# Conditioning chunks and sample-state outputs as fp32 products in quarters of the array's columns

## The chip, the cores and the metric

One core of one Trainium2 chip runs the whole program. The metric is the device time of one execution in microseconds; the kernel before is shown with the median of three executions. One further execution was profiled, and all rows below are of it.

## The reference, cut to what matters

One layer of a conditioned hybrid decoder (RG-LRU and gated linear attention side by side, merged by gates, then a SwiGLU block) is computed for a prompt of 1024 tokens and for eight sample sequences of four tokens. Two places matter here.

The conditioning: each of the nine sequences (one prompt, eight samples) has a vector `c`, from which six vectors of 1024 modulate the layer:

```
mod = silu(c) @ ada_w + ada_b                  # (9, 1024) @ (1024, 6144)
sh1, sc1, gt1, sh2, sc2, gt2 = split(mod, 6)
h  = rmsnorm(x, norm1_g) * (1 + sc1) + sh1
...
x  = x + gt1 * (m @ w_out)
h2 = rmsnorm(x, norm2_g) * (1 + sc2) + sh2
x  = x + gt2 * (ffn(h2))
```

The sample sequences' attention output, per head, from a state `S` that each of the eight sequences brings along (128 x 256 for each head), with four tokens each:

```
o = att @ v + (q * exp(b)) @ S                 # per sequence: (4, 128) @ (128, 256)
S = exp(b_last) * S + (k * exp(b_last - b)).T @ v
```

## The kernel before, in words

The 1056 token rows are worked in two halves: A (512 prompt rows) and B (512 prompt rows and the 32 sample rows). Features lie on the 128 partitions, tokens along the free dimension. Every large product takes its weights as a tile of 128 x 1024 fp32 that is split in two fp32r parts: `load_w` (L121) loads the raw tile through the SP queue into one of three `raw` buffers, ScalarE writes the high part (L125), VectorE the remainder (L126), into one of three `hl` buffers. A product is then three fp32r products (L358 to L360).

The conditioning is cut into twelve chunks of 512 outputs, each with four weight tiles of 128 x 1024 (two contraction tiles of 512 columns in each). Chunks 2, 0, 3 and 1 are needed first and are made at the start by `ada_first` (L169): the raw fp32 tiles go into `S` buffers (pool `sbig`, 17 of them, shared with most of the large intermediate tiles), and each of the eight contraction tiles is one fp32 product of 32 stationary columns against 512 moving ones, written to one of four 32-partition quarters of a PSUM bank (L178). ScalarE copies the bank out (L181), and four products with a 0/1 matrix `sel` add the four quarters and transpose (L184); VectorE adds the bias (L186).

The other eight chunks (4 to 11) are made by `ada_chunk` (L218) with split weights through `load_w`, against a stationary `cst` of 128 columns that holds the high part of the conditioning in columns 0 to 8 and its remainder in 32 to 40 (`ada_split`, L208; `cst` keeps one `S` buffer): sixteen fp32r products of 512 columns (L226), a copy (L196), four transposes (L198), two VectorE operations (L201, L202).

Python generators set the order of the work. `ada_rest` (L244) runs chunks 4 to 11 one after the other and gives a step at each `yield`: five for a chunk, 40 in all. `weave` (L300) lets one or two such steps follow each tile of another generator: one after each step of `qk(1)` and of `values(1)`, two after each of the eight tiles of `r_tiles` (L798), and one at each step of `merge_b` (L935). `mix` (L310) then lays these fillers between the steps of the attention generator `gla` (L565), by the credits that the yields state. This happens in half A alone. Instructions of one engine run in the order in which they stand, the DMA issues of the SP queue too. PSUM banks for short use come from `ax` (L79), a pool of two.

In half B, `gla` makes the sample part for each of four heads: two loads bring the states (L746, `s0b`, two `S` buffers); eight fp32 products, one for each sequence, of 32 stationary columns (`qmb`) against 256 state columns add up in one 32-row PSUM area (L751), and one of 32 rows for the sequences' own tokens is added (L752). ScalarE copies out (L754), two transposes follow (L766), ScalarE copies the result into `ob` (L767). Between them stand the products for the new state (L758) and VectorE's update (L762).

Of the kernel before, what the change touches and what calls it, by code (L numbers as in the profile page):

```python
# [9 lines left out]
I32 = mybir.dt.int32  # L10
AF = mybir.ActivationFunctionType
OP = mybir.AluOpType
PSUM = bass.MemoryType.PSUM

P = 128
# [31 lines left out]
def hybrid_layer(ctx, tc, I, O):  # L47
# [11 lines left out]
    def S(name, dt=F32):  # L59
        return sbig.tile([P, 2 * 544], dt, tag="S", name=name)  # L60
# [29 lines left out]
    pool.dma_start(lmask, I["lmask"])  # L90
    bmask = cp.tile([P, NB], F32, name="bmask")
    pool.dma_start(bmask, I["bmask"])
    sel = cp.tile([P, 9], F32, name="sel")
    pool.dma_start(sel, I["sel"])
    hlru0 = cp.tile([P, NR, NB], F32, name="hlru0")
    pool.dma_start(hlru0, I["slru"])
    sconv = cp.tile([P, NR, NB, 3], F32, name="sconv")
# [68 lines left out]
    act.activation(cth[:, :, 0:9], ct, AF.Tanh, scale=0.5)  # L166
    dve.scalar_tensor_tensor(cth[:, :, 0:9], cth[:, :, 0:9], 1.0, ct, op0=OP.add, op1=OP.mult)

    def ada_first(cc):  # L169

        ps = ax(f"adaps{cc}")
        for kk in range(4):
            raw = S(f"ada{cc}{kk}")
            sp.dma_start(raw[:, :1024], I["ada_w"][cc, kk])
            for i in range(2):
                kt = 2 * kk + i
                g = 32 * (kt % 4)
                pe.matmul(ps[g:g + 32, :], cth[:, kt, :], raw[:, i * 512:(i + 1) * 512], start=(kt < 4), stop=(kt >= 4))  # L178
            yield 1.0
        row = T(f"adar{cc}")  # L180
        act.activation(row[:, :512], ps, AF.Copy)  # L181
        tps = ax(f"adat{cc}")
        for i in range(4):
            pe.matmul(tps[:, i * 16:i * 16 + 9], row[:, i * P:(i + 1) * P], sel, start=True, stop=True)  # L184
        mo = mod[:, 4 * cc:4 * cc + 4, :]
        dve.scalar_tensor_tensor(mo, tps[:, :64].rearrange("p (j m) -> p j m", m=16)[:, :, 0:9], 0.5, ada_bias(cc),  # L186
                                 op0=OP.mult, op1=OP.add)
        ada_derive(cc, mo)
        yield 1.0

    def ada_bias(cc):
        return bc(vec[:, V_ADAB + 4 * cc:V_ADAB + 4 * cc + 4].unsqueeze(2), [P, 4, 9])

    def ada_out(cc, ps, tps, row):
        n = 41
        act.activation(row[:n, :512], ps[:n], AF.Copy)  # L196
        for i in range(4):
            pe.transpose(tps[:, i * 64:i * 64 + n], row[:n, i * P:(i + 1) * P], ident[:n, :n])  # L198
        t3 = tps[:, :256].rearrange("p (j m) -> p j m", m=64)
        mo = mod[:, 4 * cc:4 * cc + 4, :]  # L200
        dve.scalar_tensor_tensor(mo, t3[:, :, 0:9], 0.5, ada_bias(cc), op0=OP.mult, op1=OP.add)  # L201
        dve.scalar_tensor_tensor(mo, t3[:, :, 32:41], 0.5, mo, op0=OP.mult, op1=OP.add)  # L202
        ada_derive(cc, mo)


    cst = []

    def ada_split():  # L208
        zz = S("zz")
        pool.memset(zz, 0.0)  # L210
        cw = S("cst", F32R)
        dve.tensor_copy(cw, zz)
        c3 = cw[:, :KD * P].rearrange("p (k m) -> p k m", m=P)
        dve.tensor_copy(c3[:, :, 0:9], cth[:, :, 0:9])
        dve.tensor_sub(c3[:, :, 32:41], cth[:, :, 0:9], c3[:, :, 0:9].bitcast(F32))
        cst.extend(c3[:, i, :] for i in range(KD))

    def ada_chunk(cc):  # L218

        ps = ax(f"adaps{cc}")  # L220
        for kk in range(4):
            w = load_w(I["ada_w"][cc, kk], 1024, f"ada{cc}{kk}")
            for i in range(2):
                kt = 2 * kk + i
                for u in range(2):
                    pe.matmul(ps, cst[kt], w[:, u, i * 512:(i + 1) * 512], start=(kt == 0 and u == 0),  # L226
                              stop=(kt == KD - 1 and u == 1))
            yield 0.87
        yield 0.5
        ada_out(cc, ps, ax(f"adat{cc}"), T(f"adar{cc}"))  # L230

    def ada_derive(cc, mo):
        ch, j = cc // 2, 4 * (cc % 2)
# [86 lines left out]
    class Half:  # L320
# [129 lines left out]
        def norm1(s):  # L450
            box = s.rb1
            s.h = []
            for q in range(2):
                if s.hf == 0 and q:
                    s.lr_half(0)
                    for i, t in enumerate((T_Q, T_Q + 1, T_K, T_K + 1)):
                        hl = load_w(I["w_in"][t], 1024, f"early{t}") if i < 3 else load_apart(I["w_in"][t], f"early{t}")
                        ps = mm(f"early{t}")
                        s.gemm(ps, hl, 4, s.h, 0, True, False)
                        s.early[t] = ps, hl  # L460
                    for cc in (3, 1):
                        yield from ada_first(cc)
                yield from s.modulate(s.h, s.xs, box[0], s.whole, range(4 * q, 4 * q + 4), 0, 0, "1" + s.n)


# [99 lines left out]
        def gla(s, pr, z, q, k, vg, vts):  # L565
# [125 lines left out]
            for i in range(2):  # L691
# [33 lines left out]
                if s.hf:  # L725
                    pool.dma_start(O["gla_p"][:, h, :], st_prev)
                    vs = vts[2 * i + 1]
                    kr = tp.tile([P, 4, NS], F32R, tag="vr", name=f"kr{n}{i}", bufs=2)
                    kes = bc(ke[:, i * N + HP:i * N + N].unsqueeze(1), [P, 2, NS])
                    dve.tensor_copy(kr[:, 0:2, :], kes)  # L730
                    dve.tensor_sub(kr[:, 2:4, :], kes, kr[:, 0:2, :].bitcast(F32))
                    qt = T(f"qm{n}{i}")
                    qm = qt[:, :NB * NS].rearrange("p (b j) -> p b j", b=NB)
                    dve.memset(qm, 0.0)
                    dve.tensor_copy(qt[:, :NB * 36].rearrange("p (b j) -> p b j", j=36)[:, :, 0:TS],
                                    qe[:, i * N + HP:i * N + N].rearrange("p (b j) -> p b j", j=TS))
                    yield 1
                    tps = ax(f"ktq{n}{i}")
                    pe.transpose(tps[:, :P], kr.rearrange("p a b -> p (a b)").bitcast(F32), ident)
                    kem = S(f"kem{n}{i}", F32R)  # L740
                    dve.tensor_mul(kem[:, :1024].rearrange("p (b k) -> p b k", b=NB), bc(tps[:, :P].unsqueeze(1), [P, NB, P]),
                                   bc(bmask.unsqueeze(2), [P, NB, P]))
                    sts = []
                    for g in range(2):
                        s0 = S(f"s0{n}{i}{g}")
                        sp.dma_start(s0[:, :1024], I["sgla"][h, :, g * 1024:(g + 1) * 1024])  # L746
                        sts.append(s0)
                    yield 2
                    pos = ax(f"pos{n}{i}")
                    for b in range(NB):  # L750
                        pe.matmul(pos[:NS, :256], qm[:, b, :], sts[b // 4][:, (b % 4) * 256:(b % 4 + 1) * 256], start=(b == 0), stop=False)  # L751
                    pe.matmul(pos[:NS, :256], atts[:, i * NS:(i + 1) * NS], vs[0], start=False, stop=True)  # L752
                    osb = T(f"osb{n}{i}")[:NS, :256]
                    act.activation(osb, pos[:NS, :256], AF.Copy)  # L754
                    for b in range(0, NB, 2):
                        ups = ax(f"upt{n}{i}{b}")
                        for d in range(2):
                            pe.matmul(ups[:, d * 256:(d + 1) * 256], kem[:, (b + d) * P:(b + d + 1) * P], vs[1], start=True, stop=True)  # L758
                        for d in range(2):
                            sv = sts[(b + d) // 4][:, ((b + d) % 4) * 256:((b + d) % 4 + 1) * 256]  # L760
                            ec = i * N + HP + (b + d) * TS + TS - 1
                            dve.scalar_tensor_tensor(sv, sv, e0[:, ec:ec + 1], ups[:, d * 256:(d + 1) * 256], op0=OP.mult, op1=OP.add)  # L762
                        yield 1
                    pot = ax(f"pot{n}{i}")
                    for v in range(2):
                        pe.transpose(pot[:, v * NS:(v + 1) * NS], osb[:, v * P:(v + 1) * P], ident[:NS, :NS])  # L766
                    act.activation(o3[:, :, HP:], pot[:, :2 * NS].rearrange("p (v j) -> p v j", v=2), AF.Copy)  # L767
                    for g in range(2):
                        pool.dma_start(O["gla_s"][h, :, g * 1024:(g + 1) * 1024], sts[g][:, :1024])
                os_.append(ot)  # L770
# [364 lines left out]
    mm_pool(1)  # L1135
    A.load_x()
    drain(A.norm1_sum())
    drain(ada_first(2))
    drain(ada_first(0))
    drain(A.norm1())  # L1140
    ada_split()
    derive()
    A.branches(None)
    up1 = A.ffn1(1)
# [41 lines left out]
def _pack(inp):  # L1186
# [40 lines left out]
    jj = np.arange(P)[:, None]  # L1227
    ii = np.arange(64)[None, :]
    a["lmask"] = np.stack([((jj // (2 * b) == ii // b) & (jj % (2 * b) < b)) for b in LEVELS], 1).astype(np.float32)
    a["sel"] = (np.arange(P)[:, None] % 32 == np.arange(9)[None, :]).astype(np.float32)  # L1230
    a["bmask"] = (np.arange(P)[:, None] % NS // TS == np.arange(NB)[None, :]).astype(np.float32)
    return a

# [27 lines left out]
```

## Time and profile before

| | |
|---|---|
| median of 3 executions | 2069.88 us (2068.68 to 2071.18) |
| the profiled execution | 2071.19 us |
| its span, first to last instruction | 2069.4 us |
| mean granted TensorE clock | 0.993 |
| PE / PEld busy | 2022.4 / 1835.9 us |
| VectorE (DVE) / ScalarE (ACT) busy | 1132.5 / 831.5 us |
| DMA | 228.39 MB, mean 110 GB/s |

Times are microseconds from the first instruction unless marked ns. PE is TensorE's products, PEld its weight loads, POOL is GpSimd, SP the queue that issues most loads. A product's recorded duration includes the time in which its last columns leave the array, so the distance from one start to the next is what it costs. fp32 products stand as two instructions each, fp32r products and transposes as one.

### The profile page before, as it was taken

How to read it: one execution, taken by the hardware profiler on the slowest of the kernel's cores; microseconds unless marked ns; L12 is line 12 of the kernel's file. 1: busy time of each engine (PE TensorE's matmuls, PEld its weight loads, DVE VectorE, ACT ScalarE, POOL GpSimd, SP SyncE). 2: the span in 40 equal slices, each digit the busy share in tenths (PEclk: the TensorE clock that was granted, in tenths of full speed). 3: DMA queues.
4: the chain of work that ended last, by engine and by line, in shares of the span. 5: the costliest groups of instructions: out<-in, count | busy, mean ns of one | idle time of the engine just before them, and what ended most of it. 6: DMA issues, size and time to landing. Idle time of an engine off the chain costs nothing. (4 is left out here: it accounts for less than half of the span.)

```text
span 2069.4 us, 31495 instructions
## 1 busy us (share of the span) xinstructions
PE 2022.4 (98%) x13106; PEld 1835.9 (89%) x13106; DVE 1132.5 (55%) x1795; ACT 831.5 (40%) x1153; POOL 85.3 (4%) x136
## 2 busy tenths in 40 slices
PE   6999999999999999999999999999999999999997
PEld 4787887788899888888899898899999999999997
DVE  4757767655347433446564597684243673333356
ACT  3536456645235322233352345563232442212232
POOL 1101001000000000000010011110000000000000
PEclk9999999999999999999999999999999999999999
DMA  7233423433344423342422313322233542232234
GB/s 284 79 111 94 138 76 116 134 122 110 98 154 148 133 79 105 102 139 72 152 69 85 115 48 105 107 78 96 79 96 99 166 136 94 75 107 86 90 114 126
DMA packets 74270, 228.39 MB, mean 110 GB/s; under 512 B 8496, under 2 KB 16304, under 8 KB 74128
## 3 DMA queue, kind: packets, MB, share of 16 engines
q1 hardware_dynamic: 70960, 216.98, 32.6%
q0 software_dynamic: 2624, 8.85, 1.2%
q8 instruction: 103, 1.69, 0.3%
q10 hardware_dynamic: 544, 0.56, 0.1%
q14 instruction: 39, 0.32, 0.0%
HBM read 217.12 MB, written 9.23 MB: 109 GB/s over the span
## 5 line engine op out<-in xcount | busy, mean ns | idle before, releaser
L360 PE MATMUL f3psb<-fab,f3b_hl 128*128 128x272 f32 x352 | 101.4, 288 | 0.0
L358 PE MATMUL f3psb<-fab,f3b_hl 128*128 128x272 f32 x352 | 101.3, 288 | 0.0
L359 PE MATMUL f3psb<-fab,f3b_hl 128*128 128x272 f32 x352 | 100.9, 287 | 0.0
L125 ACT ACTIVATE f3b_hl<-f3b_raw 128x768 fp32r<-128x768 f32 (+1 forms) x45 | 35.7, 793 | 88.4 <-PE f3psb L360 56.1
L358 PE MATMUL f3psa<-faa,f3a_hl 128*128 128x512 f32 x176 | 68.7, 390 | 0.0
L360 PE MATMUL f3psa<-faa,f3a_hl 128*128 128x512 f32 x176 | 68.5, 389 | 0.0
L359 PE MATMUL f3psa<-faa,f3a_hl 128*128 128x512 f32 x176 | 68.5, 389 | 0.0
L358 PEld LDWEIGHTS f3psb<-fab,f3b_hl 128*128 128x128 f32 x352 | 66.4, 189 | 0.0
L360 PEld LDWEIGHTS f3psb<-fab,f3b_hl 128*128 128x128 f32 x352 | 66.2, 188 | 0.0
L359 PEld LDWEIGHTS f3psb<-fab,f3b_hl 128*128 128x128 f32 x352 | 66.1, 188 | 0.0
L126 DVE TENSOR_TENSOR f3b_hl<-f3b_raw,f3b_hl 128x768 fp32r<-128x768 f32 (+1 forms) x45 | 40.1, 892 | 35.1 <-ACT f3b_hl L125 34.9
L125 ACT ACTIVATE f3a_hl<-f3a_raw 128x768 fp32r<-128x768 f32 (+1 forms) x32 | 25.4, 793 | 84.2 <-PE f3psa L360 46.4
L126 DVE TENSOR_TENSOR ada_hl<-ada_raw,ada_hl 128x1024 fp32r<-128x1024 f32 x32 | 38.9, 1222 | 24.8 <-ACT ada_hl L125 24.6
L126 DVE TENSOR_TENSOR f3a_hl<-f3a_raw,f3a_hl 128x768 fp32r<-128x768 f32 (+1 forms) x32 | 28.5, 890 | 39.0 <-ACT f3a_hl L125 38.3
L125 ACT ACTIVATE ada_hl<-ada_raw 128x1024 fp32r<-128x1024 f32 x32 | 33.5, 1054 | 35.6 <-PE vpsa L360 13.1
L358 PE MATMUL uxpsb<-h1b,uxpsb_hl 128*128 128x272 f32 x160 | 47.4, 296 | 0.0
L360 PE MATMUL uxpsb<-h1b,uxpsb_hl 128*128 128x272 f32 x160 | 46.2, 289 | 0.0
L358 PE MATMUL ugpsb<-h1b,ugpsb_hl 128*128 128x272 f32 x160 | 46.2, 289 | 0.0
L359 PE MATMUL uxpsb<-h1b,uxpsb_hl 128*128 128x272 f32 x160 | 46.1, 288 | 0.0
L360 PE MATMUL ugpsb<-h1b,ugpsb_hl 128*128 128x272 f32 x160 | 46.0, 288 | 0.0
L359 PE MATMUL ugpsb<-h1b,ugpsb_hl 128*128 128x272 f32 x160 | 45.8, 286 | 0.0
L360 PEld LDWEIGHTS f3psa<-faa,f3a_hl 128*128 128x128 f32 x176 | 33.0, 188 | 7.1 <-DVE f3a_hl L126 0.2
(1491 smaller groups left out, 7248.5 us busy)
## 6 DMA issues: line engine op xcount, KB each, us to landing
ada_raw<-in_ada_w SPq DMA_DIRECT2D x32, 512.0 KB, 3.6
f3b_raw<-in_ffn SPq DMA_DIRECT2D x23, 384.0 KB, 3.1
ada<-in_ada_w SPq DMA_DIRECT2D x16, 512.0 KB, 10.0
f3b_raw<-in_ffn SPq DMA_DIRECT2D x22, 320.0 KB, 2.9
woa_raw<-in_w_out SPq DMA_DIRECT2D x13, 512.0 KB, 3.4
wob_raw<-in_w_out SPq DMA_DIRECT2D x13, 512.0 KB, 3.3
f3a_raw<-in_ffn SPq DMA_DIRECT2D x16, 384.0 KB, 3.1
uxpsa_raw<-in_w_in SPq DMA_DIRECT2D x10, 512.0 KB, 3.6
```

The costliest lines, as they stand in the source:

```text
L125: act.activation(hl[:, 0, :n], raw[:, :n], AF.Copy)
L126: dve.tensor_sub(hl[:, 1, :n], raw[:, :n], hl[:, 0, :n].bitcast(F32))
L358: pe.matmul(out, wh, x[:, o:o + w], start=st, stop=False)
L359: pe.matmul(out, wh, x[:, N + o:N + o + w], start=False, stop=False)
L360: pe.matmul(out, wl, x[:, o:o + w], start=False, stop=en)
```

## The change

`ada_first` and the old `ada_chunk` become one `ada_chunk`, used for all twelve chunks: raw fp32 tiles in `S` buffers, loaded two at a time, eight fp32 products in quarters for each chunk, a copy of the bank, four transposes of 128 x 128, a VectorE reduction over the four quarters, and one VectorE operation for the bias. `cst`, `ada_split` and `sel` are gone. A chunk has three steps in place of five. The sample-state products go to four quarters in the same way (sequence b to quarter b mod 4, the own-token product to the last), and the quarters are added by a VectorE reduction after the transposes in place of ScalarE's copy.

```diff
-    sel = cp.tile([P, 9], F32, name="sel")
-    pool.dma_start(sel, I["sel"])
...
-    def ada_first(cc):
...
+    def groups(t, n):
+
+        return t.rearrange("p (j g m) -> p j m g", g=4, m=32)[:, :, 0:n, :]
+
+    def ada_load(cc, k0, k1):
+        raws = []
+        for kk in range(k0, k1):
             raw = S(f"ada{cc}{kk}")
             sp.dma_start(raw[:, :1024], I["ada_w"][cc, kk])
+            raws.append(raw)
+        return raws
+
+    def ada_chunk(cc, raws=None):
+
+        ps = ax(f"adaps{cc}")
+        for kk in range(0, 4, 2):
+            two = raws[kk:kk + 2] if raws else ada_load(cc, kk, kk + 2)
+            for g in range(4):
+                pe.matmul(ps[32 * g:32 * g + 32, :], cth[:, 2 * kk + g, :], two[g // 2][:, (g % 2) * 512:(g % 2 + 1) * 512],
+                          start=(kk == 0), stop=(kk == 2))
             yield 1.0
         row = T(f"adar{cc}")
         act.activation(row[:, :512], ps, AF.Copy)
         tps = ax(f"adat{cc}")
         for i in range(4):
-            pe.matmul(tps[:, i * 16:i * 16 + 9], row[:, i * P:(i + 1) * P], sel, start=True, stop=True)
+            pe.transpose(tps[:, i * P:(i + 1) * P], row[:, i * P:(i + 1) * P], ident)
         mo = mod[:, 4 * cc:4 * cc + 4, :]
-        dve.scalar_tensor_tensor(mo, tps[:, :64].rearrange("p (j m) -> p j m", m=16)[:, :, 0:9], 0.5, ada_bias(cc),
+        dve.tensor_reduce(mo, groups(tps, 9), axis=AX.X, op=OP.add)
+        dve.scalar_tensor_tensor(mo, mo, 0.5, bc(vec[:, V_ADAB + 4 * cc:V_ADAB + 4 * cc + 4].unsqueeze(2), [P, 4, 9]),
                                  op0=OP.mult, op1=OP.add)
         ada_derive(cc, mo)
-        yield 1.0
...
-    def ada_split():
...
-    def ada_chunk(cc):
...
-            yield 0.87
         yield 0.5
-        ada_out(cc, ps, ax(f"adat{cc}"), T(f"adar{cc}"))
...
                     for b in range(NB):
-                        pe.matmul(pos[:NS, :256], qm[:, b, :], sts[b // 4][:, (b % 4) * 256:(b % 4 + 1) * 256], start=(b == 0), stop=False)
-                    pe.matmul(pos[:NS, :256], atts[:, i * NS:(i + 1) * NS], vs[0], start=False, stop=True)
-                    osb = T(f"osb{n}{i}")[:NS, :256]
-                    act.activation(osb, pos[:NS, :256], AF.Copy)
+                        g = 32 * (b % 4)
+                        pe.matmul(pos[g:g + 32, :256], qm[:, b, :], sts[b // 4][:, (b % 4) * 256:(b % 4 + 1) * 256], start=(b < 4),
+                                  stop=(3 < b < 7), skip_group_check=True)
+                    pe.matmul(pos[96:128, :256], atts[:, i * NS:(i + 1) * NS], vs[0], start=False, stop=True, skip_group_check=True)
+                    osb = T(f"osb{n}{i}")[:, :256]
+                    act.activation(osb, pos[:, :256], AF.Copy)
...
-                        pe.transpose(pot[:, v * NS:(v + 1) * NS], osb[:, v * P:(v + 1) * P], ident[:NS, :NS])
-                    act.activation(o3[:, :, HP:], pot[:, :2 * NS].rearrange("p (v j) -> p v j", v=2), AF.Copy)
+                        pe.transpose(pot[:, v * P:(v + 1) * P], osb[:, v * P:(v + 1) * P], ident)
+                    dve.tensor_reduce(o3[:, :, HP:], groups(pot[:, :256], NS), axis=AX.X, op=OP.add)
...
-    drain(ada_first(2))
-    drain(ada_first(0))
+    drain(ada_chunk(2))
+    drain(ada_chunk(0))
     drain(A.norm1())
-    ada_split()
```

## Rows read from the trace of the kernel before

**Rows 1.** The page, busy us of each engine (share of the span, instructions).

```profile
PE 2022.4 (98%) x13106; PEld 1835.9 (89%) x13106; DVE 1132.5 (55%) x1795; ACT 831.5 (40%) x1153; POOL 85.3 (4%) x136
```

**Rows 2.** Windows: length; busy of PE, PEld, DVE, ACT, POOL; PE clock; DMA share; GB/s.

```profile
0.00:20.00 20.00, 4.27 (x19) 4.22 (x20) 9.87 (x47) 6.24 (x11) 4.37 (x15) 1.00 0.90 334
180.00:260.00 80.00, 76.28 (x404) 63.74 (x403) 60.92 (x79) 36.04 (x45) 5.84 (x3) 0.96 0.40 127
1180.00:1220.00 40.00, 37.01 (x308) 36.18 (x307) 37.39 (x57) 19.54 (x24) 7.61 (x4) 1.00 0.20 62
187.96:194.79 6.83, 6.20 (x21) 5.32 (x22) 5.83 (x8) 3.07 (x6) 0.19 (x1) 0.50 0.07 5
```

**Rows 3.** Timeline of PE around split chunks: start, us from first start to last end.

```profile
217.38 2.11 PE L226 MATMUL adaps<-ada_hl,cst 128*128 128x512 f32 x8
...
227.50 1.98 PE L226 MATMUL adaps<-ada_hl,cst 128*128 128x512 f32 x8
229.31 1.89 PE L648 MATMUL spsa<-wa 128*128 128x64 f32 x16
...
467.30 0.44 PE L198 MATMUL adat<-ident,adar 41*128 41x41 f32 x4
467.67 1.19 PE L226 MATMUL adaps<-ada_hl,cst 128*128 128x512 f32 x4
```

**Rows 4.** Timeline of PE around the quarter products of an early chunk.

```profile
47.16 0.39 PE L359 MATMUL early<-h1a,early_hi 128*128 128x512 f32 x1
47.39 0.39 PE L360 MATMUL early<-h1a,early_lo 128*128 128x512 f32 x1
47.71 1.92 PE L178 MATMUL adaps<-ada,cth 128*32 128x512 f32 x16
50.41 1.06 PE L184 MATMUL adat<-sel,adar 128*128 128x9 f32 x8 [0.78 <-ACT adar L181]
```

**Rows 5.** Timeline of PE around the sample-state products of the first head.

```profile
1137.80 0.29 PE L358 MATMUL vpsb<-h1b,vpsb_hl 128*128 128x272 f32 x1
1137.92 0.29 PE L359 MATMUL vpsb<-h1b,vpsb_hl 128*128 128x272 f32 x1
1138.14 3.64 PE L751 MATMUL posb<-s0b,qmb 128*32 128x256 f32 x16
1141.71 0.61 PE L752 MATMUL posb<-vs,attsb 32*32 32x256 f32 x2
1142.26 0.50 PE L758 MATMUL uptb<-vr,kemb 128*128 128x256 f32 x2
```

**Rows 6.** Timeline of PE: four transposes of 128 x 128 and what follows.

```profile
1144.88 0.60 PE L533 MATMUL vtpb<-ident,vfb 128*128 128x128 f32 x4
1145.32 0.27 PE L538 MATMUL vtqb<-ident,vfb 128*32 128x128 f32 x1
```

**Rows 7.** By tile and line: count, duration ns min/median/max, first and last start.

```profile
L125 ACT ACTIVATE ada_hl<-ada_raw x32: 1039/1055/1063, 93.5 to 478.9; 128x1024 fp32r<-128x1024 f32 x32
L126 DVE TENSOR_TENSOR ada_hl<-ada_raw,ada_hl x32: 1207/1224/1241, 94.8 to 480.0; 128x1024 fp32r<-128x1024 f32 x32
L201 DVE SCALAR_TENSOR_TENSOR mod<-adat,vec x8: 188/195/196, 145.0 to 504.2; 128x36 f32<-128x36 f32 x8
L539 DVE COPY vs<-vtqb x8: 278/279/279, 1056.0 to 1153.9; 32x128 f32<-32x128 f32 x8
```

**Rows 8.** Loads of the conditioning weights, early chunks (`ada`), then split ones (`ada_raw`).

```profile
DMA to landing us min/median/max: 6.2/10.0/11.9
...
DMA to landing us min/median/max: 3.3/3.6/6.2
```

**Rows 9.** Timeline around PE's longest pause after the start: DVE, then PE.

```profile
183.33 2.87 DVE L632 TENSOR_TENSOR wa<-bca 128x512 f32<-128x512 f32 x1
...
188.59 2.08 PE L377 MATMUL rpsoa<-ident,orstda 128*128 128x128 f32 x8 [3.72 <-DVE atta L602]
```

More of the change, by code (lines that the diff above doesn't have):

```diff
@@ L12 @@
 OP = mybir.AluOpType
+AX = mybir.AxisListType
 PSUM = bass.MemoryType.PSUM
@@ L167, in hybrid_layer @@
     dve.scalar_tensor_tensor(cth[:, :, 0:9], cth[:, :, 0:9], 1.0, ct, op0=OP.add, op1=OP.mult)
-    def ada_first(cc):
-        ps = ax(f"adaps{cc}")
-        for kk in range(4):
+    def groups(t, n):
[3 more added lines that the diff above has]
+        for kk in range(k0, k1):
             raw = S(f"ada{cc}{kk}")
             sp.dma_start(raw[:, :1024], I["ada_w"][cc, kk])
[L175 to L178, printed above, removed]
+            raws.append(raw)
[7 more added lines that the diff above has]
+                          start=(kk == 0), stop=(kk == 2))
             yield 1.0
@@ L183, in ada_first @@
         for i in range(4):
-            pe.matmul(tps[:, i * 16:i * 16 + 9], row[:, i * P:(i + 1) * P], sel, start=True, stop=True)
+            pe.transpose(tps[:, i * P:(i + 1) * P], row[:, i * P:(i + 1) * P], ident)
         mo = mod[:, 4 * cc:4 * cc + 4, :]
-        dve.scalar_tensor_tensor(mo, tps[:, :64].rearrange("p (j m) -> p j m", m=16)[:, :, 0:9], 0.5, ada_bias(cc),
+        dve.tensor_reduce(mo, groups(tps, 9), axis=AX.X, op=OP.add)
+        dve.scalar_tensor_tensor(mo, mo, 0.5, bc(vec[:, V_ADAB + 4 * cc:V_ADAB + 4 * cc + 4].unsqueeze(2), [P, 4, 9]),
                                  op0=OP.mult, op1=OP.add)
         ada_derive(cc, mo)
-        yield 1.0
[L191 to L206, printed above, removed]
-    def ada_split():
[L209 to L216, printed above, removed]
-    def ada_chunk(cc):
[L220 to L227, printed above, removed]
-            yield 0.87
         yield 0.5
-        ada_out(cc, ps, ax(f"adat{cc}"), T(f"adar{cc}"))
     def ada_derive(cc, mo):
@@ L461, in norm1 @@
                     for cc in (3, 1):
-                        yield from ada_first(cc)
+                        yield from ada_chunk(cc)
                 yield from s.modulate(s.h, s.xs, box[0], s.whole, range(4 * q, 4 * q + 4), 0, 0, "1" + s.n)
@@ L1229, in _pack @@
     a["lmask"] = np.stack([((jj // (2 * b) == ii // b) & (jj % (2 * b) < b)) for b in LEVELS], 1).astype(np.float32)
-    a["sel"] = (np.arange(P)[:, None] % 32 == np.arange(9)[None, :]).astype(np.float32)
     a["bmask"] = (np.arange(P)[:, None] % NS // TS == np.arange(NB)[None, :]).astype(np.float32)
```

## The prediction, made before the changed kernel was run

> **What bounds the kernel now.** I read the page's busy times first: PE is busy in 2022.4 of 2069.4 us, VectorE in just over half, ScalarE in 40% [rows 1]. So the time is PE's, and a PE microsecond removed is a microsecond gained wherever PE doesn't begin to wait for something else. Then the windows, to see where it could: at 180 to 260 us VectorE is busy 60.92 of 80 us and PE idles 3.7; at 1180 to 1220 VectorE is busy 37.39 of 40 us, PE 37.01 [rows 2]. These are the two stretches beside the affected work with little room. Then PE's timeline at each place that the change touches, where the distance from start to start is the cost.
>
> **The eight later chunks, before.** Eight L226 products last from 227.50 to the next work at 229.31, 1.81 us (0.227 each); at 217.38 the eight are 0.246 apart ((2.11 - 0.39)/7) [rows 3]. Sixteen are 3.62 to 3.94 us. The four 41-row transposes occupy 467.30 to 467.67, 0.37 us [rows 3]. A chunk costs 3.99 to 4.31 us of PE.
>
> **The same, after.** The early chunks already show the new product: sixteen instructions in 1.92 us from first start to last end [rows 4]. One of 512 columns in fp32 takes two passes of 512, 0.43 us at 2.4 GHz (twice the 0.213 of 512 columns), so sixteen in a row would be 6.8; four run abreast. Taking off the tail of a product's record (0.39 less 0.227, so 0.16), they cost 1.76, and a half chunk of eight 0.88. Going in costs 47.71 - 47.39 - 0.227 = 0.09 us [rows 4]. Coming out is read at the sample products: the last of sixteen starts 0.213 us before 1138.14 + 3.64 - 0.38 + 0.213 = 1141.61 and the next form begins at 1141.71, so 0.10 [rows 5]. The loads of a chunk arrive in two pairs with other work between, so 2 x (0.88 + 0.19) = 2.14 us, and four transposes of 128 x 128 take 1144.88 to 1145.32, 0.44 [rows 6]. A chunk costs 2.58 us. Gain 1.41 to 1.73 each, 11.3 to 13.8 for eight; I take **12.0**, nearer the closer-spaced products, since most of the 0.246 spacing sits in one crowded stretch.
>
> TensorE drains between these forms by 0.09 to 0.10 us as the rows stand. The Trainium skill says in "TensorEngine Tiling (Array Packing)", Key Properties, that changing the tiling mode, not just the tile, drains the engine, which speaks against interleaving the forms. If that meant a whole product's tail of 0.16 us at each of the 32 new changes of form, 32 x 0.065 = 2 us of the gain would go and the sum below would end 2 us higher; rows 4 and 5 show less, so I keep them.
>
> **What leaves VectorE and ScalarE.** 32 high parts of 1.055 us on ScalarE and 32 remainders of 1.224 on VectorE [rows 7], 33.8 and 39.2 us. Both lie beside PE work, so I count them at nothing; the cover is PE's own queue. They relieve just the stretch of 180 to 260. Added on VectorE: a reduction of 144 elements per chunk. No row has this operation. Below: a 36-element operation from PSUM, 0.195; above: 0.28 for 128 elements [rows 7], continued by 0.9 ns an element, 0.29, or twice that if the strided reading halves the rate, 0.6. I take 0.3 for a chunk and 0.4 for a head (256 elements). Beside PE these too cost nothing, twelve and four times; without cover, 5 us at the most.
>
> **The four early chunks.** Eight `sel` instructions (about 1 us) become four transposes (0.44), the extra 0.3 us reduction stands in the same chain towards `mod`; a chunk moves by -0.25 to +0.1, and the early products often wait for loads anyway. Zero for the four. The `sel` load and the clearing of `cst` lie on POOL and VectorE ahead of work with slack: zero.
>
> **The loads.** 32 loads move from the three `raw` buffers to the `S` pool. In the order of its instructions the program before holds at most sixteen of the seventeen `S` buffers in this stage, `cst` among them, so at the worst point two are free now, one pair, elsewhere four and more. The SP queue is in order: a pair that waits for `S` holds the weight loads behind it, and PE's product now waits for the landing itself, with the next tile's products queued behind. In return the `raw` buffers serve the other weights alone. With three steps to a chunk, sixteen of the 24 steps fall on the eight `r` tiles: 16/24 x 16.8 MB + 4.2 MB = 15.4 MB in some 75 us, 205 GB/s, against 127 in that window now and 334 reached at the start [rows 2]. A single load lands in 3.6 us, in a burst of eight 10.0 [rows 8]; a step's `r` tile is 24 products of 0.227, 5.4 us for two steps. I take no wait, as a pair is issued at least one tile ahead whenever four buffers are free; the upper bound is a rival. In `merge_b`, where fifteen steps lay, none is left: what moves is PE work that is always ready, from a stage with VectorE work to one with more, but without its splits.
>
> **The sample-state products.** Before: from 1137.92 + 0.12 (the spacing of 1137.80 and 1137.92) to 1142.26, 4.22 us [rows 5]. After: into the form 0.10, sixteen instructions of 0.213 four abreast 0.85, a change 0.10, two more of 0.213 0.43, out 0.11: 1.59 us. The two transposes stay two, of one instruction each. Gain 2.63 for a head, **10.5** for four, less up to 1 where the loads of the states end the wait (the last head). The sum of quarters moves from ScalarE to VectorE's queue: behind it stand the state updates L762, and the next user of its PSUM bank waits for it; 0.4 us at most a head.
>
> **Sum.** 12.0 + 10.5 = 22.5 us. The profiled execution took 2071.2 us (its span and 1.8 around it), 1.3 above the median; from the median, 2069.9 - 22.5 = **2047.4 us**. With the bounds of the terms (11.3 to 13.8, 9.5 to 10.5, VectorE uncovered up to 2, early chunks -1 to +0.4) this case spans 2044 to 2051.5.
>
> **The rivals.**
> 1. *PE's pause in half A goes as well.* At 188.59 PE has waited 3.72 us for VectorE's L602, and afterwards runs at 1.2 GHz from 187.96 to 194.79 [rows 2, 9]; the pause and half of that stretch are 7.1 us. The relief of VectorE speaks for it. Against: the wait holds for one of two PSUM banks, and the VectorE operations ahead of it are long for another reason: L632 takes 2.87 us here [rows 9], and POOL's work beside it is unchanged. Time 2040.3.
> 2. *VectorE keeps the end in half B.* The first two heads end just before 1180 to 1220, where VectorE is full [rows 2]. If PE merely arrives earlier and waits, their 5.3 us are lost: 2052.7.
> 3. *Pairs land late, a little.* Half a microsecond at each of the sixteen pairs: 2055.4.
> 4. *Pairs land late, and the change is slower.* The mechanism is the `S` pool: if a pair is issued only when the pair before has given up its buffers, PE has 2.7 us of `r` tile to a step while the quickest burst load took 6.2 [rows 8], 3.5 us for each pair, 56 us in all: 2103. It decides from 22.5/16 = 1.4 us of wait for each pair on; below, the change is still faster. The count of free buffers speaks against.
> 5. *The quarters don't run abreast* beside other work, the change then not doing what it says: a chunk's products take 6.8 us for 3.6, and 26 us are lost in A with none gained in B: 2095. Rows 4 speak against it.
>
> **How the numbers follow.** The likeliest case has 0.54, rivals 1 to 5 have 0.14, 0.14, 0.10, 0.06 and 0.02. A change of order of this kind also moves pauses of one or two us elsewhere, of which PE has several, and no row tells their sign. So the range goes from near rival 1 to just beyond rivals 2 and 3: 2038 to 2057. About 0.2% (4 us) is what a measurement of this kernel can tell from no change. Faster needs less than 2065.7: the first three rivals and the forecast lie below that, rivals 4 and 5 above, rival 4 when mild between; faster 0.92, same 0.03, slower 0.05.
>
> **What would show it.** In the changed profile: eight later chunks at PE with sixteen instructions in two groups of about 0.9 us, no L226 of 128 columns and no `ada_hl` on ScalarE and VectorE; `posb` from its first product to L758 in 1.5 to 1.7 us; VectorE some 33 us less busy, ScalarE some 34; the last conditioning products before about 260 us, where the last split now ends near 480 [rows 7]; PE busy near 2000. It would be wrong if PE showed waits for DMA at the quarter products (rivals 3, 4), if PE's idle time in what is now 1180 to 1220 grew by what the heads gave (rival 2), if the pause after 180 us were gone (rival 1), or if the groups of eight took over 3 us (rival 5).

## The result, and the profile after

The changed kernel takes **2048.43 us** (median of 4 executions, 2047.57 to 2050.05) against 2070.53 of the kernel before on the same chip: ratio 0.9895, interval 0.9878 to 0.9913, 22.1 us less. The forecast was 2047.4. The profiled execution took 2047.57 us with a span of 2045.6, 23.8 below the span before. In the changed kernel most lines of half A and B stand 31 lower than before: the norm's L377 is L346, L602 is L571, L648 is L617; the quarter products are L186 and L721.

The page's busy times, the answer to [rows 1]:

```profile
PE 2001.0 (98%) x13090; PEld 1807.2 (88%) x13090; DVE 1097.5 (54%) x1768; ACT 799.7 (39%) x1117; POOL 80.7 (4%) x134
```

PE is 21.4 us less busy, most of the 23.8 us by which the profiled span is shorter; VectorE (-35.0) and ScalarE (-31.8) lost the splits, which can have given at most what left the pause below. PE is still 98% busy: it bounds the kernel as before.

The windows of [rows 2], with the stretch that is at half clock now in the last line:

```profile
180.00:260.00 80.00, 77.69 (x468) 58.52 (x467) 54.62 (x85) 31.34 (x41) 6.31 (x3) 1.00 0.49 181
1180.00:1220.00 40.00, 37.70 (x306) 37.20 (x304) 36.65 (x54) 17.44 (x24) 4.42 (x8) 0.96 0.10 34
187.96:194.79 6.83, 6.69 (x43) 4.17 (x42) 6.83 (x6) 1.20 (x2) 3.51 (x2) 1.00 0.24 77
1188.15:1191.57 3.42, 3.42 (x23) 3.30 (x21) 3.42 (x6) 2.40 (x3) 0.00 (x0) 0.50 0.00 0
```

Between 180 and 260 us the loads now run at 181 GB/s (the prediction had 205) and PE idles 2.3 us, before 3.7; between 1180 and 1220 us it idles 2.3 us, before 3.0. The stretch 187.96 to 194.79, at clock 0.50 before, has 1.00. In half B 1188.15 to 1191.57 is at 0.50; before, it was 1328.02 to 1331.43, as long.

PE's waits between 150 and 210 us in the timeline, the answer to [rows 9] (start, length, and in brackets the wait and its releaser):

```profile
187.51 1.16 PE L346 MATMUL rpsoa<-ident,orstda 128*128 128x128 f32 x8 [0.69 <-ACT rboa L349]
...
204.34 1.15 PE L617 MATMUL spsa<-wa 128*64 128x64 f32 x16 [1.48 <-DVE mod L195]
```

The pause of 3.72 us is now 0.69, and a new one of 1.48 waits for the reduction of a chunk.

PE's timeline around three kinds of conditioning groups, the answer to [rows 3]:

```profile
109.96 0.39 PE L327 MATMUL qpsa<-h1a,qpsa_hl 128*128 128x512 f32 x1
110.28 1.05 PE L186 MATMUL adaps<-ada,cth 128*32 128x512 f32 x4
111.26 1.33 PE L617 MATMUL spsa<-wa 128*128 128x64 f32 x10
...
139.25 1.07 PE L186 MATMUL adaps<-ada,cth 128*32 128x512 f32 x8
140.25 1.00 PE L617 MATMUL spsa<-wa 128*128 128x64 f32 x7
...
192.70 1.92 PE L186 MATMUL adaps<-ada,cth 128*32 128x512 f32 x16
194.56 0.50 PE L327 MATMUL rpsa<-h1a,rpsa_hl 128*128 128x512 f32 x1
```

This is what the forecast did not have. A **set** (a run of quarter products with nothing between) of 16 instructions, a whole chunk, costs 1.86 us from its start to the next. A set of 8, half a chunk on four quarters, costs 1.00. A set of 4, one load on two quarters, costs 0.98, as much as twice the work. The kernel writes four products in a row, but in the order in which PE ran them other products stand between: the eight later chunks are seventeen sets, eight of 4, six of 8 and three of 16. What set this order isn't shown by any row; what earlier loads do to it is tried below.

The same at the sample heads, the answer to [rows 5]: first head, then third.

```profile
1125.46 0.29 PE L328 MATMUL vpsb<-h1b,vpsb_hl 128*128 128x272 f32 x1
1125.68 0.64 PE L721 MATMUL posb<-s0b,qmb 128*32 128x256 f32 x8
1126.25 0.51 PE L729 MATMUL uptb<-vr,kemb 128*128 128x256 f32 x2
...
1127.44 0.64 PE L721 MATMUL posb<-s0b,qmb 128*32 128x256 f32 x8
1128.01 0.61 PE L723 MATMUL posb<-vs,attsb 32*32 32x256 f32 x2
1128.55 0.50 PE L729 MATMUL uptb<-vr,kemb 128*128 128x256 f32 x2
...
1260.66 1.07 PE L721 MATMUL posb<-s0b,qmb 128*32 128x256 f32 x16
1261.66 0.61 PE L723 MATMUL posb<-vs,attsb 32*32 32x256 f32 x2
1262.21 0.50 PE L729 MATMUL uptb<-vr,kemb 128*128 128x256 f32 x2
```

The third head takes 1260.66 to 1262.21, 1.55 us. The first is broken in two, 0.57 and 1.11, with one more change of form; so are the second and the fourth.

Durations by tile and line, and the landing time of the loads (min/median/max), the answers to [rows 7, 8]:

```profile
L186 PE MATMUL adaps<-ada,cth x192: 592/593/1063, 21.3 to 248.4; 128*32 128x512 f32 x192
...
L195 DVE TENSOR_REDUCE mod<-adat x12: 294/308/309, 26.1 to 256.9; 128x36 f32<-128x144 f32 x12
...
L738 DVE TENSOR_REDUCE ob<-potb x4: 418/420/421, 1134.0 to 1302.0; 128x64 f32<-128x256 f32 x4
...
DMA to landing us min/median/max: 3.6/5.6/11.4
```

### The profile page after: what moved, and what is told of

It reads as the page before. It is cut to its first block, busy times and chain, and to the rows that moved or that the text cites. A ratio compares the mean times of both kernels' runs of the same rounds, so it can differ in the third digit from the quotient of the medians.

```text
span 2045.6 us, 31343 instructions
## 1 busy us (share of the span) xinstructions
PE 2001.0 (98%) x13090; PEld 1807.2 (88%) x13090; DVE 1097.5 (54%) x1768; ACT 799.7 (39%) x1117; POOL 80.7 (4%) x134
## 4 chain that ended last, share of the span: by engine, by line
PE 90%; DVE 5%; DMA 2%; ACT 1%; issue 1%; SPq 0%; DVEq 0%; ACTq 0%
PE f3psb L327 2%; PE f3psb L329 2%; PE f3psb L328 2%; PE f3psa L327 2%; PE f3psa L328 2%; PE f3psa L329 2%; PE spsa L617 1%; PE spsb L617 1%; PE adaps L186 1%; PE papsb L327 1%; PE papsb L329 1%; PE papsb L328 1%; PE uxpsa L327 1%; PE uxpsa L329 1%; PE papsa L327 1%; PE uxpsa L328 1%
## 5 line engine op out<-in xcount | busy, mean ns | idle before, releaser
L329 PEld LDWEIGHTS f3psa<-faa,f3a_hl 128*128 128x128 f32 x176 | 33.0, 188 | 7.1 <-DVE f3a_hl L125 0.2
L327 PEld LDWEIGHTS f3psa<-faa,f3a_hl 128*128 128x128 f32 x176 | 33.1, 188 | 6.8
L328 PEld LDWEIGHTS f3psa<-faa,f3a_hl 128*128 128x128 f32 x176 | 33.1, 188 | 6.8
```

What stands on the lines that cost most here:

```text
L327: pe.matmul(out, wh, x[:, o:o + w], start=st, stop=False)
L328: pe.matmul(out, wh, x[:, N + o:N + o + w], start=False, stop=False)
L329: pe.matmul(out, wl, x[:, o:o + w], start=False, stop=en)
```

## The experiments

Eleven kernels ran with the kernel before in the same jobs (its medians there 2071.07, 2071.5 and 2072.42 us). "A ends" is the start of the first `lrpsb` product, "B ends" the start of the last `sq3b` sum, both us by the rows of these tiles; the last column has the stretches at half clock between 70 us and the end of B. Two of the eleven are repeats, told at the end. The medians of the kernel before lie up to 1.9 us apart, and "A ends" differs by up to 1.5 us between profiles in which nothing of A was edited (heads alone 1009.0 against 1010.5, head loads ahead 999.4 against 998.0), so one or two us between two kernels are no finding by themselves.

| kernel | median us | ratio and interval | A ends | B ends | at half clock, us |
|---|---|---|---|---|---|
| before | 2070.53 | | 1010.5 | 2057.9 | 6.8 in A, 3.4 in B |
| changed | 2048.43 | 0.9895 [0.9878, 0.9913] | 998.0 | 2033.6 | 3.4 in B |
| conditioning alone | 2057.07 | 0.9932 [0.9915, 0.9948] | 998.4 | 2042.6 | none |
| heads alone | 2061.79 | 0.9955 [0.994, 0.997] | 1009.0 | 2049.0 | 6.8 in A, 3 x 3.4 in B |
| one load a step | 2066.92 | 0.998 [0.997, 0.9989] | 1016.2 | 2050.6 | 3.4 in A |
| split, three steps | 2073.46 | 1.0011 [1.0001, 1.002] | 1011.8 | 2059.5 | 6.8 in A, 3.4 in B |
| chunk loads ahead | 2047.07 | 0.9885 [0.987, 0.99] | 994.9 | 2033.2 | 3.4 in A, 2 x 3.4 in B |
| head loads ahead | 2044.45 | 0.9869 [0.9855, 0.9884] | 999.4 | 2030.7 | none |
| both ahead | 2042.11 | 0.9858 [0.9844, 0.9873] | 994.9 | 2029.0 | 3.4 in A, 2 x 3.4 in B |
| two to a quarter | 2061.09 | 0.9948 [0.9932, 0.9965] | 1009.0 | 2049.8 | 2 x 3.4 in B |
| both ahead, three steps | 2038.81 | 0.9836 [0.9822, 0.985] | 992.1 | 2024.8 | 3.4 in B |


**The two halves of the change by themselves.** First the changed kernel with the old sample products:

```diff
-                        pe.matmul(pos[g:g + 32, :256], qm[:, b, :], ... start=(b < 4),
-                                  stop=(3 < b < 7), skip_group_check=True)
+                        pe.matmul(pos[:NS, :256], qm[:, b, :], ... start=(b == 0), stop=False)
...
```

(The own-token product, the copy, the transposes and the sum go back with them.)

> The conditioning part alone: the changed kernel with the sample-state products of before. Theory: the two parts add up, and the conditioning part carries the 12 us that half A became shorter, so about 12 us less than before, 2058 (2056 to 2061), with the pause near 188 us of half A down to about 2 us, and half B as before. Rival: the gains of half B hang on what half A leaves behind (order of loads, buffers), then clearly outside this range.

Then the kernel before with the new ones:

```diff
-                        pe.matmul(pos[:NS, :256], qm[:, b, :], ... start=(b == 0), stop=False)
+                        g = 32 * (b % 4)
+                        pe.matmul(pos[g:g + 32, :256], qm[:, b, :], ... start=(b < 4),
+                                  stop=(3 < b < 7), skip_group_check=True)
...
```

> The sample-state part alone: the kernel before with the quartered sample-state products and the reduction. Theory: four heads give 10.7 us of PE, the pauses of half B stay as long in sum, so 11 us less than before, 2059.5 (2057 to 2062), and half A ends when it did, 1010.5 us to the first product of half B. Rival: VectorE is full in the stretch after the second head and takes back two heads' gain, 2065.

Measured: 2057.07 and 2061.79, that is 14.0 and 9.3 below the kernel before of their job. They add up to 23.3, the whole change gave 22.1: within 1.2 us neither takes from the other. VectorE does not keep the end of half B. Conditioning alone ends A 12.1 us earlier and also runs B 3.2 us faster, where none of its edits lie; its profile lacks the stretch at half clock there.

The heads' own worth is clearer by B alone. From the end of A to the end of B the changed kernel takes 1035.6 us and conditioning alone 1044.2, 8.6 more, though the changed kernel has a stretch of 3.4 us at half clock and the other none. At half speed throughout such a stretch loses 1.7 us, an estimate, which makes it 10.3. Heads alone takes 1040.0, the kernel before 1047.4: 7.4, with two more stretches at half clock, 10.8. From the kernel before to the changed one, with one stretch in B each, B is 11.8 us shorter. One of the stretches of heads alone in its windows (columns as in [rows 2]):

```profile
1199.42:1202.84 3.42, 3.42 (x21) 3.30 (x20) 3.42 (x6) 2.12 (x3) 0.00 (x0) 0.50 0.06 15
```

**What a set costs: one load a step.** The changed kernel with its products kept to one load (two quarters) at a time and five steps to a chunk:

```diff
-        for kk in range(0, 4, 2):
-            two = raws[kk:kk + 2] if raws else ada_load(cc, kk, kk + 2)
-            for g in range(4):
...
-            yield 1.0
+        for kk in range(4):
+            raw, = ada_load(cc, kk, kk + 1)
+            for i in range(2):
+                g = 2 * (kk % 2) + i
...
+            yield 0.5
```

> The changed kernel with one load and its two products for each step, five steps to a chunk in place of three. Theory: a set of two products costs the same 1.07 us of PE as a set of four, since only two quarters are busy; 32 sets of two make 34 us for the eight later chunks in place of the 21 measured, 13 us more than the changed kernel, 2062 (2059 to 2065). Rival: the cost goes by instructions, then 32 x 0.63 = 20 us and no change, 2048. If the PSUM bank that a chunk holds over its steps is what made the pause near 188 us, that pause returns too, 3.7 us and some 3 us of half clock on top.

Measured: 2066.92, 18.5 above the changed kernel: more than the 13 of the theory, whose pause near 188 us came back in part. The later chunks became 29 sets, 26 of them of 4. The groups by line and form (busy us, mean ns of one, idle before) of the changed kernel, conditioning products and sample products:

```profile
L186 PE MATMUL adaps<-ada,cth 128*32 128x512 f32 x192 | 31.0, 634 | 0.6 <-DMA ada<-in_ada_w 0.4
...
L721 PE MATMUL posb<-s0b,qmb 128*32 128x256 f32 x64 | 4.9, 389 | 0.4 <-DMA s0b<-in_sgla 0.4
```

The conditioning products of the kernel with one load a step, and then the two longest waits in its timeline:

```profile
L187 PE MATMUL adaps<-ada,cth 128*32 128x512 f32 x192 | 40.5, 634 | 2.1 <-DMA ada<-in_ada_w 2.1
```

```profile
189.75 1.16 PE L347 MATMUL rpsoa<-ident,orstda 128*128 128x128 f32 x8 [2.71 <-DVE atta L572]
...
451.25 1.05 PE L187 MATMUL adaps<-ada,cth 128*32 128x512 f32 x4 [1.33 <-DMA ada<-in_ada_w]
```

The same 192 instructions take 9.5 us more, by their grouping alone. Twelve more entries (1.1 us), PE's longer waits between 70 us and the end of A (seven of them, 6.4 us in all, against 2.2 in the changed kernel's two) and 3.4 us at half clock (1.7 us by the estimate) bring it to 16.5 of the 18.2 us by which A ends later; the rest stays open.

**Does the pacing alone take the pause away?** The kernel before, split weights kept, three steps to a chunk:

```diff
-            yield 0.87
-        yield 0.5
+            if kk % 2:
+                yield 1.74
         ada_out(cc, ps, ax(f"adat{cc}"), T(f"adar{cc}"))
+        yield 0.5
```

> The kernel before, its split weights and products kept, with two loads for each step and three steps to a chunk as in the changed kernel. It tells what ended the pause near 188 us. Theory: the pacing, which lets a chunk give up its PSUM bank sooner; then the pause shrinks to about 2 us and the half clock after it goes, 4 to 5 us less than before, 2066. Rival: the relief of VectorE from the remainders of the conditioning weights; then the pause stays near 3.7 us and the time near 2070.

Measured: 2073.46, neither the one nor the other. The wait at the norm has gone, and PE waits for the split weights a few us later instead:

```profile
195.48 0.62 PE L226 MATMUL adaps<-ada_hl,cst 128*128 128x512 f32 x1 [2.13 <-ACT ada_hl L125]
196.99 2.07 PE L226 MATMUL adaps<-ada_hl,cst 128*128 128x512 f32 x4 [0.90 <-DVE ada_hl L126]
```

with 6.8 us at half clock behind it. So pacing moves the pause to the splits, dropping the splits with five steps leaves 2.71 us of it (the run above), and the changed kernel, which does both, leaves 0.69 and 1.48. As the run above also groups the products otherwise, the share of each isn't separated.

**Whole sets, by loads ahead.** If a set costs by its longest quarter, the cure is to have all loads there first. Chunk loads a step or two ahead of eight products in a row:

```diff
-            two = raws[kk:kk + 2] if raws else ada_load(cc, kk, kk + 2)
-            for g in range(4):
...
-            yield 1.0
+            two = ada_load(cc, kk, kk + 2)
+            raws = raws + two if raws else two
+            if kk == 0:
+                yield 0.5
+        yield 0.5
+        for kt in range(8):
+            g = kt % 4
+            pe.matmul(ps[32 * g:32 * g + 32, :], cth[:, kt, :], ...
+                      start=(kt < 4), stop=(kt >= 4))
+        yield 1.0
```

> The changed kernel, with all four loads of a later chunk issued a step or two ahead of its eight products. In the program order seven of the eight later chunks are then one unbroken set of sixteen instructions and the eighth two sets (12 and 4), where the changed kernel has seventeen sets. Theory (a set costs by its longest quarter, however many quarters are filled): 17 sets took 8 x 0.982 + 6 x 0.996 + 3 x 1.854 + 17 x 0.09 = 20.9 us; now 7 x 1.854 + 1.42 + 0.98 + 9 x 0.09 = 16.2, so 4.7 us less than the changed kernel's 2048.4: 2043.7 (2042 to 2046). Rival (the buffers of the large pool are all in use in the stretch of these chunks, so four loads held at once come late): PE waits for loads of 1 to 3 us at some chunks, or the pause near 188 us comes back with its half clock, and the time is 2047 to 2053.

Head loads a step earlier:

```diff
+                    sts = []
+                    for g in range(2):
+                        s0 = S(f"s0{n}{i}{g}")
+                        sp.dma_start(s0[:, :1024], I["sgla"][h, :, g * 1024:(g + 1) * 1024])
+                        sts.append(s0)
                     yield 1
                     tps = ax(f"ktq{n}{i}")
...
-                    sts = []
...
                     yield 2
```

> The changed kernel, with the two state loads of a sample head issued one step earlier; in the program order all four heads are then one set of eighteen instructions, where three of the four were broken in two by a pair of state updates. Theory: a broken head took 0.569 + 1.113 and one more change of form in and out (about 0.2), a whole one 1.545, so 0.34 us for each of three heads: 1.0 us less than the changed kernel, 2047.4 (2046.4 to 2048.4), with posb up to its last instruction as one row of 18 on each head. Rival (state loads held longer push other loads of the pool back): a wait for a load of 1 us or more in the half of the samples, 2049 to 2052.

and both:

> Both edits together: chunk loads ahead and head loads ahead. Theory: the two lie in different halves and add, 4.7 + 1.0 = 5.7 us less than the changed kernel: 2042.7 (2041 to 2045). Rival: the pool's late loads in either half take it back, 2047 to 2053.

Measured: 2047.07, 2044.45 and 2042.11 (expected 2043.7, 2047.4, 2042.7). Of the single ones the first gained 3.4 too little, a time in the rival's range, and the second 3.0 too much, below its own. Both ahead came as expected, but by luck: A gains 3.1 us there too and not 4.7, and B more than the 1.0. The sets themselves were as expected: 1.85 each for seven whole chunks, 1.55 for each of four heads; only the set of twelve took 1.84 instead of 1.42, as its fullest quarter holds four instructions. The rival's mechanism isn't there: PE waits for no load of a later chunk, and no pause stands near 188 us. What differs in A is the clock. With the chunk loads ahead, A ends 3.1 us earlier, not 4.7: a pause at new transposes is followed by a stretch at half clock, which would account for the difference; the timeline and the windows of that run:

```profile
168.45 0.66 PE L198 MATMUL adat<-ident,adar 128*128 128x128 f32 x4 [0.99 <-ACT adar L195]
```

```profile
171.43:174.84 3.41, 3.41 (x9) 2.67 (x8) 3.14 (x13) 0.00 (x0) 0.00 (x0) 0.50 0.10 29
1304.65:1308.07 3.42, 3.42 (x12) 2.87 (x12) 2.43 (x6) 1.97 (x4) 0.00 (x0) 0.50 0.34 108
```

and the second stretch, in B, is one that the changed kernel hadn't. Two stretches are 3.4 us by the estimate. The profile with the head loads ahead has no stretch at all, so up to 1.7 us of its gain is clock and not the edit. The rest is more than the sets. Behind the last head the changed kernel waits at L829:

```profile
1349.52 1.19 PE L829 MATMUL g1b<-xcb,lwb_raw 128*128 128x272 f32 x4 [1.16 <-DVE mbb L918]
```

This wait of the same product for `mbb`, 1.13 to 2.10 us, stands in all nine profiles without the head loads ahead and in none of the four with them. So the edit is worth more than the 1.0 that was forecast; between the two repeats told below, with one stretch in B each, B is 4.8 us shorter. How earlier loads end that wait isn't shown.

**Does the order of the quarters matter?** The changed kernel, neighbouring products on one quarter:

```diff
-                        g = 32 * (b % 4)
+                        g = 32 * (b // 2)
...
-                pe.matmul(ps[32 * g:32 * g + 32, :], cth[:, 2 * kk + g, :], ...
-                          start=(kk == 0), stop=(kk == 2))
+                q = 32 * (kk + g // 2)
+                pe.matmul(ps[q:q + 32, :], cth[:, 2 * kk + g, :], ...
+                          start=(g % 2 == 0), stop=(g % 2 == 1))
...
```

> The changed kernel with the quarters dealt in pairs: neighbouring products go to the same quarter (0, 0, 1, 1, 2, 2, 3, 3 instead of 0, 1, 2, 3, 0, 1, 2, 3), in chunks and heads; the sums are the same. Theory (each quarter keeps its own line, so only the longest chain of a set counts, whatever the order): sixteen in a row still cost 1.85, but a set of two or four products now has two of them on one quarter and costs 1.85 instead of 0.98 or 1.00. The program order has 15 sets in the later chunks, 15 x (1.85 + 0.09) = 29.1 against 20.9, plus some 0.36 for each of three broken heads: 9.3 us more than the changed kernel, 2057.7 (2055 to 2061). Rival (instructions start in order, so one that waits for its own quarter holds back all behind it): sixteen in a row take about 16 x 0.427 - 3 x 0.427 = 5.5 us, eight in two quarters 3.0, which adds 3.7 for seven whole chunks and 1.1 for seven half chunks: 2085 to 2095.

Measured: 2061.09, 12.7 above the changed kernel where the theory had 9.3 and the rival 37 or more. Its timeline (the first of these lines is two products, on one quarter; the third a whole chunk; then the first head) and its groups by line and form:

```profile
122.11 1.90 PE L187 MATMUL adaps<-ada,cth 128*32 128x512 f32 x4
123.94 0.50 PE L328 MATMUL kpsa<-h1a,kpsa_hl 128*128 128x512 f32 x1
...
199.48 1.95 PE L187 MATMUL adaps<-ada,cth 128*32 128x512 f32 x16 [0.15 <-DVE atta L572]
201.36 0.50 PE L328 MATMUL rpsa<-h1a,rpsa_hl 128*128 128x512 f32 x1
...
1136.72 1.06 PE L722 MATMUL posb<-s0b,qmb 128*32 128x256 f32 x8
1137.72 0.50 PE L730 MATMUL uptb<-vr,kemb 128*128 128x256 f32 x2
...
1138.53 1.06 PE L722 MATMUL posb<-s0b,qmb 128*32 128x256 f32 x8
1139.52 0.61 PE L724 MATMUL posb<-vs,attsb 32*32 32x256 f32 x2
```

```profile
L187 PE MATMUL adaps<-ada,cth 128*32 128x512 f32 x192 | 40.6, 626 | 0.2 <-DVE atta L572 0.2
...
L722 PE MATMUL posb<-s0b,qmb 128*32 128x256 f32 x64 | 7.5, 385 | 0.3 <-DMA s0b<-in_sgla 0.3
```

Sixteen in a row take 1.88 us in this order, 1.86 in the other. Two products on one quarter take 1.83, on two quarters 0.98. The longest quarter alone counts: two instructions on it cost 0.98, four 1.83 to 1.88. The conditioning products are busy 9.6 us more (8.2 expected) and the sample products 2.6 (1.1 expected: each of the two parts of a broken head takes 1.00 or 0.99 where it took 0.57, and the expectation counted one part a head). That is 12.2 of the 12.7.

**The best of it, and the clock once more.** All loads of a chunk in one step, products and copy in the next, transposes in the third, head loads ahead:

```diff
-        for kk in range(0, 4, 2):
-            two = raws[kk:kk + 2] if raws else ada_load(cc, kk, kk + 2)
...
-            yield 1.0
+        raws = raws or ada_load(cc, 0, 4)
+        yield 1.0
+        for kt in range(8):
...
         act.activation(row[:, :512], ps, AF.Copy)
+        yield 0.5
         tps = ax(f"adat{cc}")
...
```

> Head loads ahead as before, and a later chunk in three steps: all four loads; a step later its eight products and the copy; a step later its transposes. In the program order every one of the twelve chunks and four heads is one set. Against the version with both kinds of loads ahead (2042.1): the chunk in two sets (1.84 + 0.98 and two entries) becomes one (1.85), 1.0 us less; the pause of 1.04 us at 168.8, where the transposes came right behind their copy, goes, as the copy now has a step's time, and with it the half clock behind it (171.67 to 175.09, some 1.7 us). Theory: 2038.5 (2037 to 2041). Rival (the four loads issued at once, with no buffer to spare, land late, or the pause moves to another wait of the same length and the clock falls behind that one): 2041 to 2046.

Measured: **2038.81** (2036.95 to 2040.14), ratio 0.9836, 33.6 us below the kernel before of its job. All eight later chunks are one set, the conditioning products are busy 3.7 us less than in the changed kernel, with 0.9 us of waits for loads at the early chunks, and the window from 160 to 200 us has the full clock (groups by line and form, then the window):

```profile
L187 PE MATMUL adaps<-ada,cth 128*32 128x512 f32 x192 | 27.3, 635 | 0.9 <-DMA ada<-in_ada_w 0.9
```

```profile
160.00:200.00 40.00, 38.64 (x228) 29.46 (x227) 29.17 (x47) 22.84 (x29) 6.27 (x3) 1.00 0.43 156
```

Two kernels were run again as they were, for the clock in half B.

> The changed kernel once more, nothing edited. Its first profile showed the clock at half speed from 1188.15 to 1191.57, behind the pause of 2.30 us at 1187.8. Theory (these stretches of 3.4 us belong to a kernel's order of work): the same stretch, at the same place within 1 us, and no other between 70 and 2030; span 2045 to 2047. Rival (whether the clock falls behind a pause differs from one execution to the next): the stretch is missing or another is there, and the span moves by about 1.7 us for each.

> The version with the head loads one step ahead once more, nothing edited. Its first profile showed no stretch at half clock between 70 and 2030, though the pause of 2.30 us at 1188.6 was there. Theory (order of work): again none, span 2042 to 2043. Rival (differs between executions): one or more stretches of 3.4 us at half clock, span longer by about 1.7 us for each.

Measured: 2049.78 and 2045.14 us, one execution each. The changed kernel has its stretch again, 1188.92 to 1192.34 and no other, as the theory has it, but with a span of 2047.8 us, beyond the theory's 2047; the wait at L829 is 0.9 us longer in it. The head loads ahead had none before and have one now, as the rival has it; the span is 2043.3, 0.9 us longer and not 1.7, so the estimate of 1.7 us for a stretch holds to within a us only. The window 1180 to 1200 of that kernel, in its first profile, with the pause in the timeline, and then both in the repeat:

```profile
1180.00:1200.00 20.00, 17.70 (x152) 17.25 (x152) 19.90 (x27) 9.45 (x12) 4.12 (x4) 1.00 0.05 14
```

```profile
1188.56 1.12 PE L617 MATMUL spsb<-wb 128*64 128x64 f32 x16 [2.30 <-DVE wb L608]
```

```profile
1180.00:1200.00 20.00, 17.67 (x141) 17.17 (x140) 18.60 (x25) 9.45 (x13) 4.53 (x4) 0.91 0.04 14
```

```profile
1188.96 1.94 PE L617 MATMUL spsb<-wb 128*64 128x64 f32 x16 [2.33 <-DVE wb L608]
```

Same kernel, same pause, and the clock falls in one execution and not in the other. A difference of 1.7 us, or 3.4, between two kernels' profiles is not yet the edit's.

## Why the prediction was right, and where it was right by luck

**What bounds the kernel.** Right: 21.4 us less PE time stand beside 22.1 us less in the median; 35.0 and 31.8 us off VectorE and ScalarE gave at most what the pause below is worth.

**The heads.** Right: 10.5 us taken, 10.3 and 10.8 by B at equal clock (11.8 from the kernel before to the changed one). A whole head is 1.55 us from its first product to L729 (forecast 1.5 to 1.7). That three of four are broken in two wasn't foreseen and cost little, as each part still fills its quarters.

**The eight later chunks. This term was mis-sized: "I take 12.0", with bounds of 11.3 to 13.8.** The price of a half chunk was right: 0.88 and 0.19 forecast, 1.00 and an entry of 0.09 (110.28 less 109.96, less 0.23) measured. What failed is the sentence "the loads of a chunk arrive in two pairs with other work between, so 2 x (0.88 + 0.19)". Eight sets hold one load only, at the price of two. The seventeen sets take 8 x 0.98 + 6 x 1.00 + 3 x 1.86 = 19.4 us and 17 x 0.09 = 1.5 for the entries; with 3.8 for the transposes that is 24.7, 3.08 a chunk where the forecast had 2.58. The price before was read too low as well: the wider spacing of the products isn't a matter of one crowded stretch. The conditioning products from 70 to 1000 us, the kernel before and the changed one (columns: PE, PEld, ACT, clock, DMA share, GB/s):

```profile
70.00:1000.00 930.00, 35.96 (x128) 23.27 (x128) 4.65 (x8) 1.00 0.35 113
70.00:1000.00 930.00, 20.58 (x128) 3.35 (x128) 4.76 (x8) 1.00 0.35 115
```

Less the tail of each set (0.16 us for 30 sets before, 0.07 for 17 after) that is 31.2 and 19.4 us. So 128 products stood 0.244 us apart, and with the transposes (0.37) a chunk cost 4.27 us, 34.2 for eight. The chunks gained 34.2 - 24.7 = 9.5 us: 4.1 less than 12.0 for the price after, 1.6 more for the price before. As a check, A ends 12.5 us earlier; the pause near 188 gave 3.72 - 0.69 - 1.48 = 1.55 and the full clock half of the 6.20 us that PE worked there, 3.1 by estimate; that leaves 7.9 us, and the 1.6 us to 9.5 stay open.

**Rival 1 made it up.** The pause and its half clock, priced at 7.1 us and given 0.14, went for the greater part: 4.6 us. So the forecast holds by errors that cancel: a chunk term 2.5 us too large, a rival that came in with 4.6, and 1.6 us lost in A for which no cause is shown. By the prediction's own sign ("if the pause after 180 us were gone") rival 1 was the case. The argument against the rival (the wait holds for a bank, long operations ahead of it stay) wasn't the point: in the two runs on pacing, three steps with the splits kept move the pause to the splits, five steps without the splits keep 2.71 us of it, and the changed kernel, with three steps and no splits, leaves 0.69 and 1.48 at full clock.

**The other rivals.** Rival 2 fell: heads alone gained its full amount in B at equal clock, and PE's idle time from 1180 to 1220 us fell from 3.0 to 2.3 us. Rivals 3 and 4 didn't come: PE waited 0.4 us for conditioning loads in all, at the early chunks, with landings of 3.6 to 11.4 us; with a load a step, spread to 512 us, 2.1 us of waits appear, so the cover was real but thin. The size of the pool of `S` buffers wasn't varied. Rival 5 fell with the first set.

**Small terms.** The reductions, 0.3 and 0.4 forecast, take 0.308 and 0.420 us. They are not wholly covered: one wait of PE, 1.48 us, ends with such a reduction, and VectorE worked without a break from 199.78 us to it. Early chunks: PE's first `lrpsa` after them starts at 57.65 instead of 57.41 us, zero as taken. The rule of the Trainium skill in "TensorEngine Tiling (Array Packing)", Key Properties, that a change of mode drains the engine, agrees in kind; the measured price of entering is 0.09 us. Two more instructions on a quarter add 1.83 - 0.98 = 0.85 us, so a set of two on a quarter, 0.98, has by estimate some 0.13 for leaving. Against eight whole sets (15.6 us with their entries) the seventeen cost 5.4 us more: some 2.0 of it nine more entries and exits, 3.4 the eight half-filled sets. The half-filled set, more than the drain, was the price of interleaving.

## What to carry to other kernels

Count sets, not products: in column quarters, a run of products costs by its longest quarter and one change of form, so issue the loads early enough that all quarters are filled in one run, and look in the trace (not in the source) for whether they are. A forecast that comes out right deserves the same account as a wrong one: here a term 2.5 us too large and a pause thought to stay cancelled, and only the count by stage showed it. Before a gain of two or three us is put down to an edit, list the stretches at half clock in both profiles.

## What was not expected of the hardware

The order of products on the quarters is free within a whole set: with neighbours on one quarter (two products, four instructions each time) sixteen instructions took 1.88 us, with neighbours on different quarters 1.86. An instruction that waits for its own quarter does not hold up those behind it, at this depth. The Trainium skill says in "TensorEngine Tiling (Array Packing)", Key Properties, that tiles operate independently; these runs agree, and put a number on it.

At a pause of 2.3 us TensorE's clock went to 1.2 GHz for 3.4 us in one execution of a kernel (granted clock 0.91 from 1180 to 1200 us) and stayed at 2.4 in another (1.00). A pause of 0.99 us was followed by such a stretch 3 us later (168.45 and 171.43), the longer one of 1.48 at 204.34 by none. What decides wasn't found.
